# A decoder trunk in fp32: the seven-product scheme in one more pass of each MLP, with its products summed over passes and the SBUF tiles moved

## The chip, the core and the metric

The kernel runs on one NeuronCore of a Trainium2 chip. TensorE (PE in the profile) multiplies, VectorE (DVE) and ScalarE (ACT) work on tiles elementwise, GpSimd (POOL) does little here, and SyncE (SP) issues the DMAs that bring the weights from HBM. A tile is 128 partitions wide; PSUM, into which TensorE writes, has eight banks of 512 fp32 columns. The metric is the device time of one execution in microseconds. Before the change it is 2031.8 us, the median of three runs (2031.58 to 2032.2).

## The reference, cut to what matters

Sequence 256, width 2048, two layers. Layer 0 mixes with a gated short convolution, layer 1 with latent attention; each is followed by an MLP with 8192 hidden columns. All four blocks add to 1.414 times their input and are layer-normalised:

```python
def sq_relu_mlp(x, w1, w2):
    return jnp.square(jax.nn.relu(x @ w1)) @ w2

def reference(...):
    for layer in range(DEPTH):
        ...
        h = layer_norm(ALPHA * h + mix, ln_g[layer, 0], ln_b[layer, 0])
        h = layer_norm(ALPHA * h + sq_relu_mlp(h, mlp_w1[layer], mlp_w2[layer]),
                       ln_g[layer, 1], ln_b[layer, 1])
    return h
```

Everything is fp32. The kernel keeps that precision by splitting every operand into a rounded part (`hi`) and the rest (`lo`) and adding three products: hi by hi, hi by lo, lo by hi.

## The kernel before, in words

**Weights.** `stream` lists every piece of weight in the order of use, 512 KB each. `take` hands out the next piece and prepares those ahead of it, as long as no more than `LOOK` = 5 pieces lie ahead. `prepare` loads a piece on SP into one of five `raw` buffers, ScalarE rounds it to `hi` and VectorE subtracts to get `lo` (`split`, L116 and L117); there are eight `hi` and eight `lo` buffers. A pair of pieces for the seven-product scheme counts as three: VectorE first forms T1, T2, T3 and T4 from its blocks (L149, L152, L155), and four splits follow; T4 goes into the tile `t4` of the pool `fast`.

**An MLP** (`mlp`) runs in eight passes `q` over its hidden columns. A pass first makes eight chunks of 128 hidden columns: `products` runs 32 matmuls for each (`high` with 512 columns, L192, and `low` with 256, L196, output `ps_u`), `whole` adds the two halves of the PSUM tile, and `hidden` applies ReLU and square and splits into the tile `h` (SBUF tag `c`). Pass 0 instead takes the normalisation into the product (`mm_wide`, output `ps_w` and `ps_g`). Then the pass multiplies `h` with 1024 rows of the second weight and adds to `acc`, whose four blocks of 512 columns stand for two halves of the tokens (`block(n, t)`). `down` does this for one block of columns with 48 matmuls (`dot`, L276 to L278, output `ps_d`).

**The seven products.** In the passes of `FAST`, 1 to 6, the first two blocks of columns come from `down_fast` (output `ps_f`): seven products a step instead of eight, four steps of 21 matmuls each, 84 where two `down` would take 96. The left factors S1 to S4 are formed by VectorE in `hidden` and split into the tile `forms` (tag `a2`). `combine` then adds the seven PSUM tiles into `acc`, eleven VectorE instructions (L581, L650, L651) and one ScalarE copy.

**The last passes.** Pass 7 takes no seven products. In the first MLP it begins by preparing the residual for the next norm (`prepare_all`: sixteen VectorE instructions and one small product, `mu0p`), and ends in `to_wide`: after each block of columns its four chunks are transposed on TensorE (`turned`), added to the residual, counted for the statistics and split (`summed`); then come the first three products of the next stage (`group_of(3)`, `ps_g`), the statistics, and more products of that stage (`ps_w`). In the second MLP it ends in `to_out`: two blocks by `down`, the other two by `down_late`, which does the first half of the tokens entirely before the second. `finished` takes the statistics of each block (`bn_stats`) and, behind the last block of a half, normalises and stores that half. The gain and bias of the norm (`gbt`) are loaded on GpSimd's queue.

**Order and places.** Each engine's queue is written by the framework's planner, which gives every engine the earliest instruction in program order that its model holds to be ready; on the chip each queue then runs in that order. PSUM tiles come from two pools of four rotating banks. SBUF tiles lie one behind the other in the order in which pools and tags are first named: constants, then `xres`, `a1` and `a2` (16,512 bytes in each partition), `b` (33,024), `c` (16,384), S, Q and mu0 (1,024 each), `ab` (2,048), five `raw` buffers (4,096 each), eight `hi` and eight `lo` buffers (4,096 each), `tmp` (9,216), `small` (896), and the pool `fast` with `sf` (2,048) and `t4`.

Of the kernel before, what the change touches and what calls it, by code (L numbers as in the profile page):

```python
# [36 lines left out]
FAST = range(1, NQ - 1)  # L37
# [13 lines left out]
def trunk(ctx: ExitStack, tc: tile.TileContext, xT, vecs, w_first, w_in, w_out, w_kv, w_q, w_uk, w_uv,  # L51
# [9 lines left out]
    pmm = ctx.enter_context(tc.tile_pool(name="pmm", bufs=4, space=PS))  # L61
# [12 lines left out]
    def mlp_stream(l):  # L74
        out = []
        for q in range(NQ):
            out += halves(w1[l, q * QC:(q + 1) * QC])
            lead = 0
            if q in FAST:
                out += [(w2f[l, q, j, 0], w2f[l, q, j, 1]) for j in range(QC // 2)]  # L80
                lead = 2
            out += halves(w2[l, q, lead:])
        return out
# [6 lines left out]
    class Banks:  # L90
# [4 lines left out]
        @classmethod  # L95
        def open(cls, name):
            st = ExitStack()
            cls.more, cls.count = st.enter_context(tc.tile_pool(name=name, bufs=4, space=PS)), 0
            return st
# [30 lines left out]
    def prepare(i):  # L130
# [25 lines left out]
        f = state["fast"].tile([P, 2, BW], F32R, tag="t4", name=f"t4_{i}")  # L156
# [23 lines left out]
    def psum(name):  # L180
        return Banks.next().tile([P, 512], F32, tag="mm", name=name)
# [83 lines left out]
    def products(n, x, turned=None):  # L265

        for i in range(n):
            w = take()
            ps = psum("ps_u")
# [18 lines left out]
    def down(x, put, n):  # L288

        ps = [psum("ps_d") for _ in range(2)]  # L290
        for j in range(len(x) // 2):
            w, = take(1)
            for kk in range(2):
                k = 2 * j + kk
                for t in range(2):
                    dot(ps[t], wide_rows(w, kk), held(x[k], t), k == 0, k == len(x) - 1)
        for t in range(2):
            put(n, t, ps[t])

    def down_late(x, put, blocks):  # L300

        ws = {}
        for t in range(2):
            for n in blocks:
# [11 lines left out]
    def down_fast(x, forms):  # L316

        ps = {p: psum(f"ps_f{p}") for p, _, _ in FACTORS}
        n = len(x) // 2
        for j in range(n):  # L320
            b, = take(1)
            a = {"11": held(x[2 * j], 0), "12": held(x[2 * j + 1], 0), "22": held(x[2 * j + 1], 1)}
            for i in range(4):
                a[f"S{i + 1}"] = [forms[:, j, o, i * P:(i + 1) * P] for o in range(2)]
            for p, l, r in FACTORS:
                dot(ps[p], b[r], a[l], j == 0, j == n - 1)
        return ps
# [14 lines left out]
    cos_t = const.tile([P, T], F32, name="cos_t")  # L342
    sin_t = const.tile([P, T], F32, name="sin_t")
    mask_t = const.tile([P, 3 * P], F32, name="mask_t")
# [9 lines left out]

    def late_constants():
        nc.sync.dma_start(id_t, ident)
        nc.sync.dma_start(cos_t, cosT)
        nc.sync.dma_start(sin_t, sinT)
        nc.sync.dma_start(mask_t, mask)
# [145 lines left out]
    xres = act.tile([P, NC, T], F32, tag="xres", name="xres")  # L505
# [47 lines left out]
    late_constants()  # L553
# [3 lines left out]
    def mlp(idx, ln, blocks, fast, begin=None, extra=None):  # L557
# [24 lines left out]

        for q in range(NQ):
# [5 lines left out]
            if q == NQ - 1 and begin:  # L589
                begin()  # L590
            pair = []

            def hidden(m, ps, evac, *func):
                f = tmp.tile([P, T], F32, tag="fh", name="fh", bufs=3)
# [4 lines left out]
                put_split(h[m], f)  # L599
                pair.append(f)  # L600
                if forms is not None and m % 2:
                    (a11, a21), (a12, a22) = ((v[:, :P], v[:, P:]) for v in pair[-2:])
                    sf = fast.tile([P, 4, P], F32, tag="sf", name="sf")
# [459 lines left out]
```

## Time and profile before

| | us |
|---|---|
| median of three runs | 2031.80 |
| the profiled execution, its own time | 2031.86 |
| its span, first to last instruction | 2030.04 |
| TensorE busy | 2022.8 |
| VectorE busy | 1637.1 |
| ScalarE busy | 1186.2 |

The profile has one line for each group of instructions, with its engine, the tile written and read, the count and the mean duration. Matmuls overlap in it: one of 512 columns is shown for some 0.39 us, but the next starts 0.23 us later. What a matmul costs is therefore read from start to start in the timeline. `PEld` are the weight loads that go with each matmul.

### The profile page before, as it was taken

The page shows a single profiled execution, that of the slowest core. Times are in us where ns is not written, and L with a number is a line of the kernel's source. Part 1 is how long each engine was busy: PE and PEld are TensorE (multiplying, and loading weights), DVE is VectorE, ACT ScalarE, POOL GpSimd, SP SyncE. Part 2 cuts the span into 40 slices and gives each one's busy share as a digit, 9 for nine tenths or more (in the row PEclk, how much of TensorE's full clock was granted, in tenths as well). Part 3 has the DMA queues.
Part 4 walks back from the last instruction along what each step waited for, and adds up shares of the span by engine and source line. Part 5 has one row for each costly group of instructions (what it writes and reads, how often), then busy time and mean ns, then how long its engine had stood idle before and what let it go on. Part 6 is the DMA issues. An engine that isn't in the chain of part 4 may idle for free.

```text
span 2030.0 us, 30192 instructions
## 1 busy us (share of the span) xinstructions
PE 2022.8 (100%) x11240; PEld 1763.4 (87%) x11240; DVE 1637.1 (81%) x2559; ACT 1186.2 (58%) x1849; POOL 4.5 (0%) x25
## 2 busy tenths in 40 slices
PE   9999999999999999999999999999999999999998
PEld 8888888988888888888889998898888888888886
DVE  7667677778898988989788978776889898898966
ACT  6444445676566565655656655566656656565661
POOL 0000000000000000000000000000000000000000
PEclk9999999999999999999999999999999999999999
DMA  8666666564746557465654544656474664746573
GB/s 307 209 191 187 188 190 193 162 210 138 251 148 216 193 170 256 145 229 174 232 176 153 177 129 137 195 168 205 136 240 155 213 204 164 250 143 221 190 228 121
DMA packets 106851, 385.32 MB, mean 190 GB/s; under 512 B 11856, under 2 KB 12752, under 8 KB 106448
## 3 DMA queue, kind: packets, MB, share of 16 engines
q1 hardware_dynamic: 105984, 381.17, 57.9%
q0 software_dynamic: 576, 2.10, 0.3%
q8 instruction: 88, 1.44, 0.3%
q14 instruction: 59, 0.48, 0.1%
q10 hardware_dynamic: 144, 0.13, 0.0%
HBM read 381.25 MB, written 2.10 MB: 189 GB/s over the span
## 4 chain that ended last, share of the span: by engine, by line
PE 99%; DMA 0%; DVE 0%; issue 0%; SPq 0%; ACT 0%; DVEq 0%
PE ps_u L192 20%; PE ps_l L192 13%; PE ps_u L196 11%; PE ps_d L276 7%; PE ps_d L277 7%; PE ps_d L278 7%; PE ps_l L196 7%; PE ps_f L278 4%; PE ps_f L276 4%; PE ps_f L277 4%; PE ps_w L226 1%; PE ps_w L224 1%; PE ps_w L225 1%; PE ps_g L226 1%; PE ps_g L224 1%; PE ps_g L225 1%
## 5 line engine op out<-in xcount | busy, mean ns | idle before, releaser
L117 DVE TENSOR_TENSOR lo<-raw,hi 128x1024 fp32r<-128x1024 f32 x710 | 858.7, 1222 | 271.5 <-ACT hi L116 199.9
L116 ACT CAST hi<-raw 128x1024 fp32r<-128x1024 f32 x710 | 740.9, 1050 | 428.4 <-DMA raw<-in_w_dram 134.6
L192 PE MATMUL ps_u<-xhl,hi 128*128 128x512 f32 x1792 | 621.3, 391 | 0.0
L196 PE MATMUL ps_u<-xhl,lo 128*128 128x256 f32 x1792 | 500.1, 280 | 0.0
L192 PEld LDWEIGHTS ps_u<-xhl,hi 128*128 128x128 f32 x1792 | 334.4, 187 | 71.9
L196 PEld LDWEIGHTS ps_u<-xhl,lo 128*128 128x128 f32 x1792 | 339.2, 189 | 1.7
L276 PE MATMUL ps_d<-hi,h 128*128 128x512 f32 x640 | 249.9, 390 | 0.0
L277 PE MATMUL ps_d<-lo,h 128*128 128x512 f32 x640 | 249.3, 390 | 0.0
L278 PE MATMUL ps_d<-hi,h 128*128 128x512 f32 x640 | 249.2, 389 | 0.0
L192 PE MATMUL ps_l<-xhl_a,hi 128*128 128x512 f32 x704 | 244.1, 393 | 0.0
L196 PE MATMUL ps_l<-xhl_a,lo 128*128 128x256 f32 x704 | 195.5, 280 | 0.0
L192 PEld LDWEIGHTS ps_l<-xhl_a,hi 128*128 128x128 f32 x704 | 132.2, 188 | 29.8
L278 PEld LDWEIGHTS ps_d<-hi,h 128*128 128x128 f32 x640 | 120.2, 188 | 25.2
L276 PEld LDWEIGHTS ps_d<-hi,h 128*128 128x128 f32 x640 | 120.2, 188 | 25.0
L277 PEld LDWEIGHTS ps_d<-lo,h 128*128 128x128 f32 x640 | 120.2, 188 | 24.6
L196 PEld LDWEIGHTS ps_l<-xhl_a,lo 128*128 128x128 f32 x704 | 131.9, 188 | 0.2
L597 ACT ACTIVATE fh<-fh 128x256 f32<-128x256 f32 x112 | 46.5, 415 | 89.2 <-DVE fh L333 89.1
L116 ACT CAST hi_t<-raw_t 128x1024 fp32r<-128x1024 f32 x48 | 50.6, 1054 | 55.5 <-DVE raw_t L149 30.5
L192 PE MATMUL ps_l<-z,hi 128*128 128x512 f32 x240 | 82.4, 391 | 0.0
L226 PE MATMUL ps_w<-xd,hi 128*128 128x258 f32 x256 | 72.7, 285 | 0.0
L224 PE MATMUL ps_w<-xd,hi 128*128 128x258 f32 x256 | 72.6, 284 | 0.0
L225 PE MATMUL ps_w<-xd,lo 128*128 128x258 f32 x256 | 72.4, 283 | 0.0
(253 smaller groups left out, 3185.1 us busy)
## 6 DMA issues: line engine op xcount, KB each, us to landing
raw<-in_w_dram SPq DMA_DIRECT2D x416, 512.0 KB, 4.3
raw<-in_w2f_dram SPq DMA_DIRECT2D x96, 512.0 KB, 3.5
raw<-in_w_in_dram SPq DMA_DIRECT2D x88, 512.0 KB, 3.8
raw<-in_w_out_dram SPq DMA_DIRECT2D x32, 512.0 KB, 3.6
raw<-in_w_o_dram SPq DMA_DIRECT2D x32, 512.0 KB, 4.0
raw<-in_w_kv_dram SPq DMA_DIRECT2D x10, 512.0 KB, 3.6
raw<-in_w_q_dram SPq DMA_DIRECT2D x8, 512.0 KB, 4.4
raw<-in_w_uk_dram SPq DMA_DIRECT2D x8, 512.0 KB, 4.6
```

What stands on the lines that cost most here:

```text
L116: nc.scalar.copy(hi, src)
L117: nc.vector.tensor_tensor(lo, src, hi.bitcast(F32), ALU.subtract)
L192: nc.tensor.matmul(ps, w[blk // 8][0][:, blk % 8, :], x, start=first, stop=False)
L196: nc.tensor.matmul(ps[:, :T], w[blk // 8][1][:, blk % 8, :], x[:, :T], start=False, stop=last)
L224: nc.tensor.matmul(ps[:, :W], hi, x[k][:, :W], start=k == 0, stop=False)
L225: nc.tensor.matmul(ps[:, :W], lo, x[k][:, :W], start=False, stop=False)
L226: nc.tensor.matmul(ps[:, :W], hi, x[k][:, W:], start=False, stop=k == NC - 1)
L276: nc.tensor.matmul(ps, x[0], w[0], start=first, stop=False)
L277: nc.tensor.matmul(ps, x[0], w[1], start=False, stop=False)
L278: nc.tensor.matmul(ps, x[1], w[0], start=False, stop=last)
L597: nc.scalar.activation(f, f, AF.Relu)
```

## The change

`FAST` now takes in pass 7. The seven products of a pass are no longer combined in the pass: those that enter one block alone (2, 3 and 4) are added to `acc`, and the other four are kept in a new tile `sums`, added up over the passes 1 to 7; `fold` combines them once, in the last pass, with six VectorE instructions. The order of the seven products in a step is new, and every PSUM tile of the passes from 1 on has its bank written out. The forms and the splits of `h` are made for two chunks at a time. Preparing the residual is spread over the chunks of pass 7. In `to_wide` and `to_out` the first two blocks are ready after the fold, so that `down` and `down_late` do the other two; `gbt` is loaded on SP's queue. The tags of the large SBUF tiles are named at the start with unused columns between them, the cosine, sine and mask tables go to the attention's pool, and the region that the framework reserves for GpSimd's DMAs is cut to 4,096 bytes.

```diff
-FAST = range(1, NQ - 1)
+FAST = range(1, NQ)
...
+    xres = act.tile([P, NC, T], F32, tag="xres", name="xres")
+    for tag, columns in (("c", 4096), ("pad0", 64), ("b", 8256), ("a1", 4128), ("pad1", 96), ("a2", 4128), ("pad2", 96)):
+        act.tile([P, columns], F32, tag=tag, name=f"at_{tag}")
+    small.tile([P, 32], F32, tag="pad", name="at_pad", bufs=1)
...
-            return cls.more if cls.more is not None and cls.count % 8 >= 4 else pmm
+            return (cls.count - 1) % (4 if cls.more is None else 8)
...
-        f = state["fast"].tile([P, 2, BW], F32R, tag="t4", name=f"t4_{i}")
+        f = state["fast"].tile([P, 2, BW], F32R, tag="t4", name=f"t4_{i}", bufs=2)
...
-    def down(x, put, n):
+    def down(x, put, n, banks=(None, None), amid=None):
...
+            if amid and 2 * j + 2 == len(x) // 2:
+                amid()
...
-    FACTORS = (("4", "22", "T4"), ("2", "12", "21"), ("3", "S4", "22"), ("1", "11", "11"),
-               ("6", "S2", "T2"), ("7", "S3", "T3"), ("5", "S1", "T1"))
+    OWN, KEPT = ("1", "5", "7", "6"), (2, 3, 4, 5, 6, 7, 0)
+    FACTORS = (("3", "S4", "22"), ("1", "11", "11"), ("5", "S1", "T1"), ("7", "S3", "T3"),
+               ("2", "12", "21"), ("6", "S2", "T2"), ("4", "22", "T4"))
...
+        sums = fast.tile([P, 4, BW], F32, name=f"sums{idx}")
+        def keep(p, ps):
+            at = sums[:, OWN.index(p)] if p in OWN else block(*{"2": (0, 0), "3": (1, 0), "4": (0, 1)}[p])
+            if q == 0 or q == FAST[0] and p in OWN:
+                nc.scalar.copy(at, ps)
+            else:
+                nc.vector.tensor_tensor(at, at, ps, ALU.add)
+        def first_pair(h, forms, banks):
+            n = QC // 2
+            ps = {p: psum(f"ps_f{p}", bank) for (p, _, _), bank in zip(FACTORS, banks)}
+            for j in range(n):
+                fast_products(ps, h, forms, j, n)
+            for p in ps:
+                keep(p, ps[p])
+        def fold():
+            s1, s5, s7, s6 = (sums[:, i] for i in range(4))
+            both = acc[:, 1, :2 * BW].rearrange("p (b c) -> p b c", b=2)
+            right = acc[:, :, BW:2 * BW]
+            two = lambda v: v.unsqueeze(1).to_broadcast([P, 2, BW])
+            for d, a, b in ((block(0, 0), block(0, 0), s1), (s6, s6, s1), (block(1, 0), block(1, 0), s6),
+                            (s7, s7, s6), (both, both, two(s7)), (right, right, two(s5))):
+                nc.vector.tensor_tensor(d, a, b, ALU.add)
+                yield
...
-            if q == NQ - 1 and begin:
-                begin()
...
+                if begin:
+                    begin(range(1))
...
-                for m, ps in enumerate(products(QC, xhl, turned=None if q == NQ - 1 and begin else TURNED)):
+                for m, ps in enumerate(products(QC, xhl, TURNED, (0, 1))):
                     hidden(m, ps, whole)
+                    if q == NQ - 1:
+                        if begin:
+                            begin(range(max(2 * m, 1), 2 * m + 2))
             if q == NQ - 1:
-                blocks(block, put, h)
+                first_pair(h, forms, KEPT)
+                blocks(block, put, h, fold)
                 return
-            if q in FAST:
-                combine(put, down_fast(h, forms))
-            for n in range(2 if q in FAST else 0, NB):
-                if n == NB - 1 and extra:
-                    extra(block, q - 1)
-                down(h, put, n)
+            if q == 0:
+                for n in range(NB):
+                    down(h, put, n)
+            else:
+                first_pair(h, forms, KEPT)
+                for n, banks in ((2, (1, 2)), (3, (3, 4))):
+                    down(h, put, n, banks)
+                    if extra and n == 2 and q <= NB:
+                        for t in range(2):
+                            extra(block, q - 1, t, 5 + t)
...
-        for n in range(NB):
-            down(h, put, n)
-            if n:
-                turned(n - 1)
+        for _ in fold():
+            pass
+        down(h, put, 2, (1, 2))
+        turned(0)
+        down(h, put, 3, (3, 4), lambda: turned(1))
+        turned(2)
         ln.ws = group_of(GROUP)
...
-            nc.gpsimd.dma_start(gbt[:, n, :], gb[n].partition_broadcast(P))
+            nc.sync.dma_start(gbt[:, n, :], gb[n].partition_broadcast(P))
...
+        for _ in fold():
+            pass
         for n in range(2):
-            down(h, finished, n)
+            for t in range(2):
+                finished(n, t)
         down_late(h, finished, range(2, NB))
...
-    nc = _bacc.Bacc("TRN2", target_bir_lowering=False, num_devices=1)
+    nc = _bacc.Bacc("TRN2", target_bir_lowering=False, num_devices=1, dynamic_dma_scratch_size=4096)
```

More of the change, by code (lines that the diff above doesn't have):

```diff
@@ L178, in take, with psum @@
         return [ready.pop(i + j) for j in range(halves)]
-    def psum(name):
-        return Banks.next().tile([P, 512], F32, tag="mm", name=name)
+    def psum(name, bank=None):
+        bank = Banks.next() if bank is None else bank
+        return (pmm if bank < 4 else Banks.more).tile([P, 512], F32, tag=f"mm{bank}", name=name)
     def high_early(ps, w, blk, x, last):
@@ L552, in trunk @@
                 ln.prepare(k)
-    late_constants()
+    nc.sync.dma_start(id_t, ident)
     ln.widen("a1", "a2")
```

129 lines of the change are left out of this document (58 added, 71 removed).

## The prediction

> **What bounds the kernel now.** The page's busy times and its chain of waits came first:
>
> ```profile
> PE 2022.8 (100%) x11240; PEld 1763.4 (87%) x11240; DVE 1637.1 (81%) x2559; ACT 1186.2 (58%) x1849; POOL 4.5 (0%) x25
> ...
> PE 99%; DMA 0%; DVE 0%; issue 0%; SPq 0%; ACT 0%; DVEq 0%
> ```
>
> TensorE is the path from end to end, so work taken from other engines is worth nothing by itself; VectorE at 81% is near enough to become the path where work is pushed together. Next, busy times by stage: a seven-product part and the plain blocks behind it (pass 6, first MLP), the last pass of the first MLP (products, two blocks, two blocks with transposes, next stage), the last four blocks of the second MLP, and the tail. Columns: window, length, busy time of PE, PEld, DVE, ACT, POOL with counts, clock, DMA share, GB/s.
>
> ```profile
> 927.76:947.35 19.59, 19.59 (x86) 15.78 (x85) 18.15 (x24) 12.85 (x18) 0.53 (x1) 1.00 0.60 186
> 947.35:969.15 21.80, 21.80 (x97) 18.02 (x96) 19.09 (x23) 10.50 (x11) 0.00 (x0) 1.00 0.75 256
> 969.15:1013.97 44.82, 44.82 (x260) 39.55 (x259) 32.13 (x50) 27.45 (x46) 0.00 (x0) 1.00 0.67 223
> 1013.97:1035.77 21.80, 21.80 (x98) 17.98 (x97) 12.15 (x15) 9.84 (x13) 0.00 (x0) 1.00 0.63 193
> 1035.77:1060.12 24.35, 24.35 (x121) 20.47 (x120) 23.28 (x45) 15.04 (x25) 0.00 (x0) 1.00 0.50 162
> 1060.12:1080.42 20.30, 20.27 (x169) 20.06 (x168) 16.24 (x37) 9.66 (x22) 0.00 (x0) 1.00 0.42 144
> 1975.63:2019.19 43.56, 43.56 (x194) 36.07 (x193) 28.48 (x43) 10.98 (x14) 2.23 (x4) 1.00 0.36 133
> 2019.19:2030.00 10.81, 5.58 (x13) 2.00 (x11) 6.26 (x14) 0.20 (x1) 0.00 (x0) 1.00 0.26 97
> ```
>
> Seven products take 19.59 us for 84 matmuls, 233.2 ns each; two plain blocks 21.80 us for 96, 227.1 ns. VectorE has 18.15 of 19.59 us there, but only 12.15 of 21.80 in the last pass's first two blocks: that spare is what the change spends. Last, the timeline of TensorE and VectorE (start, duration, engine, line, tiles):
>
> ```profile
> 946.42 0.40 PE L278 MATMUL ps_f<-hi_t,forms 128*128 128x512 f32 x1
> 946.65 0.39 PE L276 MATMUL ps_f<-hi_t,forms 128*128 128x512 f32 x1
> 946.88 0.40 PE L277 MATMUL ps_f<-lo_t,forms 128*128 128x512 f32 x1
> 947.12 0.39 PE L278 MATMUL ps_f<-hi_t,forms 128*128 128x512 f32 x1
> ...
> 949.20 0.39 PE L278 MATMUL ps_d<-hi,h 128*128 128x512 f32 x1
> 949.43 0.39 PE L276 MATMUL ps_d<-hi,h 128*128 128x512 f32 x1
> 949.65 0.39 PE L277 MATMUL ps_d<-lo,h 128*128 128x512 f32 x1
> ```
>
> ```profile
> 945.25 0.68 DVE L581 TENSOR_TENSOR acc<-acc,ps_f 128x512 f32<-128x512 f32 x1
> ...
> 1035.47 1.28 DVE L581 TENSOR_TENSOR acc<-acc,ps_d 128x512 f32<-128x512 f32 x2
> ...
> 1055.20 2.36 DVE L117 TENSOR_TENSOR lo<-raw,hi 128x1024 fp32r<-128x1024 f32 x2
> ```
>
> From start to start a seven-product matmul takes 229 and 237 ns in turn, a plain one 226 to 227, after some ten matmuls of settling. VectorE's costs are read the same way: a second add of 512 columns adds 1.28 - 0.68 = 0.60 us, a second split of 1024 columns 2.36 - 1.22 = 1.14.
>
> **The change part by part**, against the profiled execution's 2031.86 us (the median of the runs is 2031.80).
>
> *Places in SBUF.* Nothing waits in the seven products, yet they pay 6 ns a matmul. What sets them apart is where operands start. Summing the tile sizes, `h` (tag c) and all hi and lo buffers agree modulo 512 bytes (16,384 + 3,072 + 2,048 + 20,480 = 82 x 512). `forms` in a2 is 128 bytes off (16,512 + 33,024 leaves 384), and `t4` 128 off (65,536 + 9,216 + 896 + 2,048 leaves 384). Stages whose operands keep one distance, `ps_d` and `ps_u`, run steadily. After the change a2 lies 130 x 512 bytes behind c and 83 x 512 ahead of hi, and `t4` 168 x 512 behind hi (65,536 + 7,168 + 1,024 + 8,192 + 2,048 + 2,048): all agree. b keeps its distance to hi, 256 modulo 512. So I take plain pace, 226.9 ns x 84 = 19.06 us, in the twelve parts there were: 12 x 0.53 = -6.4 us. Ends: no effect, or +6.9 us if all took the slowest spacing inside a step, 240 ns (500.25 to 500.49). The first stage reads a1 and a2, also 128 bytes apart today; its pairs settle within 2 ns of the steady 347: -0.2 us, between -0.8 and 0.
>
> *Last passes.* Two plain blocks, 96 x 226.9 = 21.78 us, become 19.06: 2 x -2.72 = -5.4 us. The last pass of the first MLP also gets the order of the others (44.57 against 44.39 us): -0.2. The small product of the residual, 0.24 us, only moves.
>
> *Kept sums.* Seven adds a pass in place of eleven and a copy: 2.4 us of VectorE less, nothing on the path, since TensorE already hid them. The written-out banks cost nothing in passes 1 to 6: the first sum is added before its bank is taken, and a product's bank comes up again 5.5 us after it ends, against 0.8 for its evacuation. Spreading sixteen preparations adds some 5 us to a VectorE that has 7 spare in the products' 44.4.
>
> *End of the first MLP.* Let T be the end of the last seven products. VectorE's list up to the statistics: two splits and seven adds, begun 2.1 us before T as at 945.25, end at T + 4.4. Then fold 4 x 0.60 + 2 x 1.14 = 4.7; ten splits 11.4; four adds of `ps_d` 2.4; four `summed` at 5.67 (1060.23 to 1065.90) 22.7: T + 45.6, and 0.8 to the statistics, 46.4. TensorE's own list is 21.8 + 4 x 0.79 (`turned`) + 17.4 (`ps_g`) = 42.4. Of the 4.0 us between, the 1.9 us of `ps_w` that the planner pulls ahead here today cover a part: +2.1 us. Ends: 0 if VectorE gains its lead earlier; 6 if two further splits go first and nothing covers. Queued behind the fold are the splits of the next weights, and TensorE waits for those (the sixth piece at T + 10.2 against its need at T + 14, the third unit of `ps_g` later than its need).
>
> *End of the second MLP.* VectorE again, from T + 4.4: fold 4.7; four `bn_stats` and two gains 3.6; three splits 3.4; add and statistics of the third block 1.4; the whole end of the first half 7.5 (2008.51 to 2016.02); add, statistics and gain of the second half 2.1: T + 27.1. The last add started today at 2019.39 and the span ended 10.65 later: T + 37.8. TensorE alone would allow 21.8 + 10.85 = T + 32.6. So +5.2 us. Ends: 0 if the splits slip in earlier and the lists overlap; 8 if `gbt`, 2 MB moved from GpSimd's queue to SP's among the weights' loads (9.5 us to landing today), makes those late. Storing, the tables moved to the attention's pool (0.5 MB, used 60 us later) and the smaller reserve hang on nothing late.
>
> Sum: -6.4 - 0.2 - 5.4 - 0.2 + 2.1 + 5.2 = -4.9, **2027.0 us**; own range 2023.5 to 2030.5 from the two ends.
>
> **The rivals.** (1) *VectorE's lists are hidden*: both ends as TensorE allows, 2027.0 - 7.3 = 2019.7, with half of them 2023. For: VectorE idles 7 us in each pass's products. Against: at most five pieces may be prepared ahead, so that idle time can't be used early.
>
> (2) *The tiles' places do nothing*: the seven products stay at 19.59. Then -2 x 2.19 - 0.2 + 7.3 = +2.7, 2034.6. For: no row shows an address, and the step also changes banks and left factors with every product. Against: `ps_g` changes banks as often and keeps its pace, and the seven products reach no steady spacing even over nine matmuls that all read `forms`. [...]
>
> (3) *The other side: the moved tiles unsettle the 1808 matmuls of 512 columns in `ps_u`, which read b.* The distance b to hi goes from 768 to 1792 modulo 2048; if that counts and not modulo 512, `ps_u` may fall into the spacing of the seven products: 1808 x 6.3 ns = 11.4 us, 2038.4. It ends the gain from 780 such matmuls on, and makes the kernel slower by over 0.2% from 1,430. Against: the left operands of `ps_d` lie at all four multiples of 512 within 2048, at one pace.
>
> **How the numbers follow.** 0.2%, 4.1 us, is about what a measurement of this kernel tells from no change. Forecast 0.50 (0.33 of it under 2027.7, the rest within), (1) 0.15, all faster, (2) 0.20, half of it over 2035.9 if the ends also cost more, (3) 0.12, slower, something else 0.03. Faster 0.48, within 0.28, slower 0.24. The range 2021.0 to 2035.5 leaves out (3) and the edges of (1) and (2).
>
> **What would show it.** Right: `ps_f` parts of about 19.06 us, fourteen of them; `ps_u` at 173.4 ns a matmul as now; VectorE without a gap behind the last seven products, TensorE waiting for `hi` or `lo` in `ps_g` and in the last blocks. Wrong: `ps_f` still at 233; `ps_u` or `ps_d` at another pace; TensorE waiting inside the seven products of pass 7, where loads or preparations would be late; or a tail as long as today's 10.8 us.

## The result and the profile after

The changed kernel takes 2037.8 us (median of eight runs, 2036.3 to 2041.4) against 2031.9 us (eight runs, 2031.6 to 2032.2): a ratio of 1.003, 95% interval 1.0021 to 1.004. It is slower by 0.3%, where 2027.0 us and a gain were forecast. The profiled execution is the shortest of the eight, 2036.3 us with a span of 2034.5; what lies between it and the median is taken up below, with the clock.

The page of the changed kernel, busy times and the sum of its chain of waits:

```profile
PE 2017.1 (99%) x11216; PEld 1758.5 (86%) x11216; DVE 1650.0 (81%) x2545; ACT 1188.0 (58%) x1813; POOL 2.3 (0%) x21
...
PE 93%; DVE 4%; DMA 1%; issue 1%; ACT 1%; SPq 0%; ACTq 0%; DVEq 0%
```

TensorE is busy 5.7 us less than before, as it should be with 24 matmuls fewer and a better pace, and the span is 4.5 us longer. It is no longer the chain from end to end: VectorE holds 4% of it, some 80 us, where it held none. The same stretches as before (columns as there: window, length, PE, PEld, DVE, ACT and POOL busy, clock, DMA share, GB/s); the last passes are split where T, the end of the last seven products, lies:

```profile
926.37:945.46 19.09, 19.09 (x87) 15.77 (x86) 18.04 (x25) 12.37 (x17) 0.00 (x0) 1.00 0.53 163
945.46:967.22 21.76, 21.76 (x98) 18.02 (x97) 18.83 (x21) 11.46 (x11) 0.00 (x0) 1.00 0.86 318
967.22:1011.61 44.39, 44.39 (x258) 39.13 (x257) 35.29 (x52) 27.57 (x45) 0.00 (x0) 1.00 0.51 156
1011.61:1030.69 19.08, 19.08 (x87) 15.77 (x85) 17.68 (x26) 12.41 (x18) 0.00 (x0) 1.00 0.54 160
1030.69:1055.42 24.73, 24.02 (x113) 19.39 (x112) 23.64 (x38) 13.45 (x18) 0.53 (x1) 1.00 0.62 209
1055.42:1084.08 28.66, 25.56 (x206) 24.50 (x205) 28.30 (x60) 15.20 (x32) 0.00 (x0) 1.00 0.52 175
1084.08:1116.78 32.70, 32.03 (x267) 31.64 (x265) 31.18 (x74) 24.73 (x51) 0.00 (x0) 1.00 0.50 157
1974.62:1993.70 19.08, 19.08 (x86) 15.77 (x85) 17.58 (x25) 12.26 (x16) 0.00 (x0) 1.00 0.80 276
1993.70:2017.78 24.08, 23.27 (x99) 18.11 (x98) 23.76 (x38) 4.41 (x5) 0.00 (x0) 1.00 0.12 49
2017.78:2034.50 16.72, 7.37 (x11) 2.42 (x9) 9.90 (x21) 0.20 (x1) 0.00 (x0) 0.78 0.33 125
```

A seven-product part is 19.08 us in pass 6 and in both last passes. Behind it, from 1030.69 on, VectorE is busy 23.64 of 24.73, 28.30 of 28.66 and 31.18 of 32.70 us, while TensorE falls short by 0.7, 3.1 and 0.7 us: VectorE is the bound there, as the experiments confirm. The last line has a granted clock of 0.78.

From start to start a seven-product matmul now takes 227 ns, with `h` and with `forms` alike (timeline of TensorE):

```profile
929.36 0.39 PE L284 MATMUL ps_f<-lo,h 128*128 128x512 f32 x1
929.59 0.39 PE L285 MATMUL ps_f<-hi,h 128*128 128x512 f32 x1
929.82 0.39 PE L283 MATMUL ps_f<-hi,forms 128*128 128x512 f32 x1
930.04 0.39 PE L284 MATMUL ps_f<-lo,forms 128*128 128x512 f32 x1
```

And the two places where the time was lost, in the timelines of VectorE and TensorE:

```profile
1071.64 5.76 DVE L122 TENSOR_TENSOR lo<-raw,hi 128x1024 fp32r<-128x1024 f32 x5
1077.31 0.75 DVE L491 TENSOR_TENSOR xres<-xres,turned 128x256 f32<-128x256 f32 x2
...
2021.42 0.68 DVE L578 TENSOR_TENSOR acc<-acc,ps_d 128x512 f32<-128x512 f32 x1
...
2025.14 5.49 PE L1000 MATMUL offset<-gbt,udiag 128*128 128x512 f32 x6 [5.48 <-DVE udiag L998]
2027.25 0.75 DVE L984 SCALAR_TENSOR_TENSOR acc<-acc,rr,offset 128x512 f32<-128x512 f32 x1 [1.51 <-PE offset L1000]
```

Five splits in a row stand ahead of the last transposed block (1077.31). At the very end the last add starts 3.6 us after the last `ps_d` (2017.78), TensorE waits 5.48 us, and the second half of its three `offset` products then takes 5.49 us. In the kernel before it took 2.84:

```profile
2023.12 2.84 PE L961 MATMUL offset<-gbt,udiag 128*128 128x512 f32 x6 [1.19 <-DVE udiag L959]
```

By stages of the two profiled executions (us; the forecast column puts the prediction's terms where they fall):

| stretch | before | after | difference | forecast |
|---|---|---|---|---|
| start to the first product on z | 274.43 | 273.65 | -0.78 | -0.2 |
| 512 products on z | 88.79 | 90.43 | +1.64 | 0 |
| up to the end of the last `ps_u`, first MLP | 650.74 | 647.53 | -3.21 | -3.4 |
| end of the first MLP, up to the first `ps_k` | 101.92 | 105.17 | +3.25 | -0.6 |
| attention and what follows it | 206.00 | 207.31 | +1.31 | 0 |
| up to the end of the last `ps_u`, second MLP | 653.75 | 650.53 | -3.22 | -3.2 |
| end of the second MLP | 54.41 | 59.88 | +5.47 | +2.5 |
| sum | 2030.04 | 2034.50 | +4.46 | -4.9 |

The passes gave what was forecast. Three stretches did not: both ends, with what follows the first, and the products on z.

### The profile page after: what moved, and what is told of

Its sections match the earlier page's. It is cut to its first block, busy times and chain, and to the rows that moved or that the text cites. A ratio compares the mean times of both kernels' runs of the same rounds, so it can differ in the third digit from the quotient of the medians.

```text
span 2034.5 us, 30102 instructions
## 1 busy us (share of the span) xinstructions
PE 2017.1 (99%) x11216; PEld 1758.5 (86%) x11216; DVE 1650.0 (81%) x2545; ACT 1188.0 (58%) x1813; POOL 2.3 (0%) x21
## 3 DMA queue, kind: packets, MB, share of 16 engines
q8 instruction: 88, 1.44, 0.3%
## 4 chain that ended last, share of the span: by engine, by line
PE 93%; DVE 4%; DMA 1%; issue 1%; ACT 1%; SPq 0%; ACTq 0%; DVEq 0%
PE ps_u L199 20%; PE ps_l L199 13%; PE ps_u L203 11%; PE ps_l L203 7%; PE ps_d L283 6%; PE ps_d L284 6%; PE ps_d L285 6%; PE ps_f L284 4%; PE ps_f L285 4%; PE ps_f L283 4%; DVE lo L122 1%; PE ps_w L233 1%; PE ps_w L232 1%; PE ps_w L231 1%; PE ps_g L231 1%
## 5 line engine op out<-in xcount | busy, mean ns | idle before, releaser
L283 PE MATMUL ps_d<-hi,h 128*128 128x512 f32 x576 | 224.8, 391 | 0.8 <-DVE sums L588 0.8
L285 PE MATMUL ps_d<-hi,h 128*128 128x512 f32 x576 | 224.3, 389 | 0.0
L284 PE MATMUL ps_d<-lo,h 128*128 128x512 f32 x576 | 224.2, 389 | 0.0
L283 PEld LDWEIGHTS ps_d<-hi,h 128*128 128x128 f32 x576 | 108.1, 188 | 23.8 <-ACT hi L121 1.6
L284 PEld LDWEIGHTS ps_d<-lo,h 128*128 128x128 f32 x576 | 108.1, 188 | 22.8 <-DVE lo L122 0.6
L285 PEld LDWEIGHTS ps_d<-hi,h 128*128 128x128 f32 x576 | 108.1, 188 | 22.5
L641 ACT ACTIVATE fp<-fp 128x256 f32<-128x256 f32 x112 | 46.7, 417 | 89.4 <-DVE fp L340 88.7
L121 ACT CAST hi_t<-raw_t 128x1024 fp32r<-128x1024 f32 x56 | 58.8, 1050 | 46.4 <-DVE raw_t L154 38.8
L154 DVE TENSOR_TENSOR raw_t<-raw,raw 128x1024 f32<-128x1024 f32 x56 | 68.3, 1220 | 8.1 <-DMA raw<-in_w2f_dram 8.0
L233 PE MATMUL ps_w<-xd,hi 128*128 128x258 f32 x256 | 72.9, 285 | 0.0
```

Source lines behind the costliest of these rows:

```text
L121: nc.scalar.copy(hi, src)
L154: nc.vector.tensor_tensor(t.rearrange(two, a=2), b12.unsqueeze(1).to_broadcast([P, 2, BW]), r1.rearrange(two, a=2), ALU.subtract)
L233: nc.tensor.matmul(ps[:, :W], hi, x[k][:, W:], start=False, stop=k == NC - 1)
L283: nc.tensor.matmul(ps, x[0], w[0], start=first, stop=False)
L284: nc.tensor.matmul(ps, x[0], w[1], start=False, stop=False)
L285: nc.tensor.matmul(ps, x[1], w[0], start=False, stop=last)
```

## The experiments

### The last passes, both, one and the other

Three kernels take the seven products out of both last passes, or of one. Only the set of passes differs (the empty one below, `(0,)` and `(1,)` for the other two), and where a last pass goes back to plain blocks the fold is spread over its chunks:

```diff
-FAST = range(1, NQ)
+FAST = [range(1, NQ if l in () else NQ - 1) for l in range(2)]
...
+                        if q not in passes:
+                            next(folding, None)
```

> The changed kernel with the seven products taken out of both last passes again; the kept sums, the written-out banks and the moved tiles stay, and the fold goes, one addition a chunk, into the products of pass 7. Theory A (both ends pay for the seven products there, by VectorE's list): the stages that the two traces share lose 0.78 + 3.28 + 3.28 + 0.43 us and gain 1.64 + 0.05 + 0.2 + 0.07, so 2031.86 - 5.8 = 2026.0 us, about 10 under the changed kernel's profiled 2036.3, and the ends stand as in the kernel before: about 101.9 us from the last ps_u of the first MLP to the first ps_k, 54.4 us behind the last ps_u of the second. Rival (the loss lies in the kept sums or the banks, not in the last passes): ends of 105 and 59 us as in the changed kernel, and 2036 + 5.4 = over 2035 us.

> The seven products in the last pass of the first MLP alone. Theory A, the two ends independent: 2026.0 + 3.26 (end of the first MLP) + 1.30 (first stages of the attention) = 2030.6 us, the end of the second MLP 54.4 us. Rival (the attention's 1.30 us comes from the moved tables or tiles and not from VectorE's backlog): 2029.3 here, and the 1.30 us stands in the kernel without either too. Rival (the profiled time is not typical: the runs of the changed kernel were 2036.3 to 2041.4): if that spread comes from the first end, this kernel shows it.

> The seven products in the last pass of the second MLP alone. Theory A: 2026.0 + 5.47 = 2031.5 us in the profiled execution, 59.9 us behind the last ps_u, a wait of 5.5 us of TensorE in the tail and a granted clock of 0.5 there; and if the clock in the tail makes the runs spread, this kernel spreads by some 5 us between runs and its median lies 1 to 2 us over its fastest. Rival (the spread is elsewhere): runs within 1 us.

| seven products in the last pass of | median (runs) us | first end | attention | second end |
|---|---|---|---|---|
| neither | 2026.36 (2026.16 to 2026.55) | 101.68 | 206.04 | 54.23 |
| the first MLP | 2032.34 (2031.30 to 2035.21) | 105.26 | 207.28 | 54.24 |
| the second MLP | 2032.06 (2030.27 to 2032.78) | 101.79 | 206.03 | 59.78 |
| both | 2037.77 (2036.3 to 2041.4) | 105.17 | 207.31 | 59.88 |

The kernel without them lies 0.4 us from the expected 2026.0 and is faster than before (ratio 0.9972, 0.9961 to 0.9982). The profiled executions of the other two, 2031.3 and 2032.06, meet 2030.6 and 2031.5 within 0.7. The ends are independent and add up; the kept sums, the banks and the places are not what costs. The attention's 1.3 us comes and goes with the first end, so it is VectorE's backlog and not the moved tables; 1.0 us of it is a wait of TensorE for a tile of VectorE's (`kqva`) that the kernel before and the one with neither don't have. The stretches of the kernel with neither, from the last `ps_u` of the first MLP to the statistics and from the last `ps_u` of the second MLP to the last `ps_d`, show TensorE almost without a gap:

```profile
1011.89:1078.48 66.59, 66.56 (x384) 58.40 (x383) 51.86 (x95) 34.77 (x59) 0.00 (x0) 1.00 0.53 166
1970.14:2013.70 43.56, 43.56 (x194) 36.04 (x193) 28.46 (x43) 10.99 (x14) 0.00 (x0) 1.00 0.37 133
```

VectorE has 14.7 us spare in the first and 15.1 in the second: that was the cover that the change spent. The spread between runs was expected of the second end; the first one has the larger (3.9 against 2.5 us), and the kernel without either has 0.4. With the first end alone, six runs of 2031.30 to 2032.34 have a mean granted clock of 1.000 and five of 2033.38 to 2035.21 one of 0.999.

### The clock in the tail

```diff
             for i, ps in enumerate(offsets):
                 nc.tensor.matmul(ps, negative, gbt[:, i, BW:], start=True, stop=False)
+            idle = psum("idle")
+            for _ in range(6):
+                nc.tensor.matmul(idle, negative, block(0, 0), start=True, stop=True)
```

> The changed kernel with six more fp32 products of 512 columns into a bank that nobody reads, behind the last ps_d and ahead of the offset products, some 0.85 us each: TensorE's 5.5 us of waiting are filled. Theory C (the clock that fell to 0.5 at 2023.7 us makes the offset products 1.71 us each in place of 0.82): the clock stays at 1.0, last add to end takes about 10.6 us in place of 13.1, 2036.3 - 2.5 = 2033.8 us, and the runs spread by 1 us or less. Rival (the wait itself is the cost, the clock only a sign of it): 2036.3 us or more, with the spread as it was.

The timeline of the kernel with the tail kept busy:

```profile
2025.72 2.84 PE L1003 MATMUL offset<-gbt,udiag 128*128 128x512 f32 x6
2026.89 2.46 DVE L984 SCALAR_TENSOR_TENSOR acc<-acc,rr,offset 128x512 f32<-128x512 f32 x3 [0.56 <-PE offset L1003]
```

The offset products are back at 2.84 us without any work being taken away (granted clock 1.00 from 2018.37 to 2028.60, where the changed kernel has 0.50 from 2023.70 to 2030.52), last add to end of span is 10.5 us in place of 13.1, the profiled execution 2034.25 (2033.8 was expected, the last add being 0.5 us later), the median 2035.52 (2034.19 to 2038.91), 2.25 us under the changed kernel's. So the slow clock behind the wait cost some 2 us. The spread stayed, 4.7 us where 1 was expected; it is not made in the tail alone, as the kernels above say too.

A second kernel takes work from VectorE ahead of the tail in place of filling TensorE's wait; it leaves out the normalisation of the first half of the tokens:

```diff
             if t == 0:
                 rsqrt(r, ve)
                 for i in range(NB):
-                    centred(i)
-                    scaled(i, us[i], gbt[:, i, BW:])
+                    store(t, i)
                 return
```

> The changed kernel, storing the first half of the tokens without its normalisation (that half of the output is left out): 8 x 0.69 = 5.5 us less on VectorE ahead of the last add. Theory B for the second end: the last add begins right behind the last ps_d, 43.9 us behind the last ps_u in place of 46.8, 2.9 us earlier, and TensorE's wait for udiag falls from 5.5 to 2.6 us. Theory C: a wait of 2.6 us leaves the clock at 1.0, another 2.5 us: last ps_u to end 56.0 - 5.4 = 50.6 us, 2031 us in the fastest runs. Rival to C (any wait of that size halves the clock): 53.1 us and 2033.4 us.

Timeline of that kernel:

```profile
2020.37 0.69 DVE L578 TENSOR_TENSOR acc<-acc,ps_d 128x512 f32<-128x512 f32 x1 [1.24 <-PE ps_d L285]
...
2024.10 2.84 PE L999 MATMUL offset<-gbt,udiag 128*128 128x512 f32 x6 [2.05 <-DVE udiag L997]
```

The last add now waits for the last product (43.72 us behind the last `ps_u`, not 46.80), TensorE's wait is 2.05 us, the granted clock is 1.00 from 2020.65 to 2026.94, and the stretch to TensorE's last instruction is 50.29 us in place of 56.01: the forecast 50.6. The median is 2032.69 us (2031.50 to 2034.68), its profiled execution 2032.63 with a granted clock of 0.98 on the mean from 1071.53 to 1141.53. Note 50.29: the kernel before has 50.33. Even with 5.5 us of VectorE's work left out the seven products win nothing at this end.

### VectorE's list in the first end

Three kernels change it: less work, another order, another engine. The first leaves out the sums of the statistics for all chunks but one.

```diff
-            nc.vector.tensor_tensor(self.S, self.S, d, ALU.add)
-            nc.vector.tensor_tensor(self.Q, self.Q, sq, ALU.add)
+            if self.idx != 1:
+                nc.vector.tensor_tensor(self.S, self.S, d, ALU.add)
+                nc.vector.tensor_tensor(self.Q, self.Q, sq, ALU.add)
```

> The changed kernel, with the sums S and Q of the second layer's first statistics left out but for the first chunk: thirty additions of 256 columns less on VectorE, 30 x 0.33 = 9.9 us, between the last seven products of the first MLP and the statistics; the normalisation that follows is not the reference's. Theory B (VectorE's list sets that end): the last ps_u to the first ps_k takes about 101.92 - 2.72 = 99.2 us in place of 105.17, the attention behind it 206.0 in place of 207.3, and 2036.3 becomes about 2029, with runs that spread by 1 us. Rival (ScalarE's copies or the weights' loads set it, VectorE only waits with them): 104 us or more, 2035 us.

Statistics at T + 41.1 in place of T + 53.4, first end 101.11 us, attention 206.04, profiled execution 2030.64, median 2031.05 (2030.10 to 2032.55). That is theory B, with 1.6 us less gain than put down. The stretches from T to the statistics and from there to `ps_k`:

```profile
1031.00:1072.12 41.12, 39.15 (x237) 34.32 (x236) 38.47 (x58) 24.36 (x40) 0.53 (x1) 1.00 0.65 215
1072.12:1113.03 40.91, 40.91 (x344) 40.91 (x343) 37.88 (x86) 30.65 (x64) 0.00 (x0) 1.00 0.55 180
```

Behind the statistics TensorE has no gap left; ahead of them it still waits 2.0 us, 0.8 of it for the fold (`turned <- DVE acc`) and 1.0 for a `lo`. These 2.0 us are what keeps 101.1 from 99.2.

The order: `take` with two pieces prepared ahead for these three units in place of `LOOK`, so that three splits move behind the statistics.

```diff
-        ln.ws = group_of(GROUP)
+        ln.ws = group_of(GROUP, 2)
```

> The changed kernel, where at the end of the first MLP the three units of the next stage (ps_g) are taken with two pieces prepared ahead in place of five: three splits of 1024 columns, 3 x 1.15 = 3.5 us of VectorE, leave the list ahead of the last transposed block; they come right behind the statistics. Theory B in its first form (the order of VectorE's list counts: what stands ahead of the last summed): statistics at T + 50 in place of T + 53.4, last ps_u to first ps_k 105.2 - 3.4 = 101.8 us, about 2033 us in the fastest runs. Theory B in its second form (the amount of VectorE's work up to ps_k counts, 31.18 us of the 32.70 between the statistics and ps_k being busy): statistics 3.4 us earlier, ps_k at most 1.5 us, over 2034.5 us. In both TensorE's wait of 1.5 us ahead of the last four chunks gets shorter, and with it the granted clock should stay at 1.0 there in every run.

Statistics at T + 50.8, 2.6 us earlier, and yet the first `ps_k` 1.3 us later (106.51 us), the median 2038.77 (2037.98 to 2040.63). The second form holds, and worse: the moved splits are wanted at once. TensorE's waits between the last seven products and the end of the projections, in the kernel with two pieces ahead (total, times, longest):

```profile
PE ps_w L232 <- DVE lo L122: 2.5, 1, 2.5
...
PE ps_g L231 <- ACT xd L426: 1.1, 3, 0.5
```

and the same in the changed kernel:

```profile
PE ps_g L231 <- ACT xd L426: 2.2, 3, 1.5
...
PE ps_w L232 <- DVE lo L122: 0.6, 1, 0.6
```

The wait for the last transposed block shrank from 1.5 to 0.5 us and one for `lo` grew from 0.6 to 2.5. Another order of a list that leaves no spare time moved the wait here.

The other engine:

```diff
-            nc.vector.tensor_tensor(self.Q, self.Q, sq, ALU.add)
+            (nc.gpsimd if self.idx == 1 else nc.vector).tensor_tensor(self.Q, self.Q, sq, ALU.add)
```

> The changed kernel with the fifteen additions to Q at the end of the first MLP on GpSimd in place of VectorE: 15 x 0.33 = 5.0 us less on VectorE. No row of the traces has a GpSimd addition; at up to four times VectorE's 0.33 us it would hide, since a chunk takes 1.4 us, and the last one would add up to 1 us ahead of the statistics. Theory B: statistics at about T + 49, last ps_u to first ps_k 101 to 102 us in place of 105.17, 2032 to 2033 us. Rival (GpSimd and VectorE hold each other up at SBUF): VectorE's additions and splits beside it take longer, and 105 us or more stay.

The first end takes 109.55 us, the median is 2041.77 (2040.57 to 2042.62): 4.0 us slower than the changed kernel, though VectorE has fifteen instructions less. Groups of instructions between 1030 and 1085 us in this kernel (GpSimd's from 1000 to 1100 us; behind the bar busy us, mean ns):

```profile
L410 POOL TENSOR_TENSOR Q<-Q,sq 128x256 f32<-128x256 f32 x15 | 14.4, 961 | 26.5 <-ACT sq L408 25.9
...
L427 DVE SCALAR_TENSOR_TENSOR xd<-xres,vec,xd 128x256 fp32r<-128x256 f32 x15 | 10.2, 680 | 1.3 <-ACT xd L426 1.3
L409 DVE TENSOR_TENSOR S<-S,xres 128x256 f32<-128x256 f32 x14 | 9.1, 648 | 0.0
```

and in the changed kernel:

```profile
L427 DVE SCALAR_TENSOR_TENSOR xd<-xres,vec,xd 128x256 fp32r<-128x256 f32 x16 | 7.7, 482 | 1.1 <-ACT xd L426 1.1
...
L409 DVE TENSOR_TENSOR S<-S,xres 128x256 f32<-128x256 f32 x15 | 6.3, 418 | 0.0
```

On the mean these two go from 418 to 648 and from 482 to 680 ns: 14 x 0.23 + 15 x 0.20 = 6.2 us, more than the 15 x 0.33 = 5.0 us that were taken away. The timeline, VectorE first and then GpSimd, shows some of them:

```profile
1057.79 1.22 DVE L122 TENSOR_TENSOR lo<-raw,hi 128x1024 fp32r<-128x1024 f32 x1
1058.93 0.95 DVE L427 SCALAR_TENSOR_TENSOR xd<-xres,vec,xd 128x256 fp32r<-128x256 f32 x1
1059.80 0.94 DVE L409 TENSOR_TENSOR S<-S,xres 128x256 f32<-128x256 f32 x1
1060.66 0.47 DVE L427 SCALAR_TENSOR_TENSOR xd<-xres,vec,xd 128x256 fp32r<-128x256 f32 x1
...
1057.86 2.60 POOL L410 TENSOR_TENSOR Q<-Q,sq 128x256 f32<-128x256 f32 x2 [2.40 <-ACT sq L408]
```

The two that begin within the 2.60 us of the GpSimd additions take 0.95 and 0.94 us; the next, which begins behind them, takes 0.47. The split at 1057.79 takes 1.22 us as in the changed kernel, though GpSimd began beside it, and all seventeen splits have a mean of 1217 ns against 1218. The two additions that begin beside that split take 2.60 us together, where two of the mean length would take 1.92. An instruction with an operand in PSUM (`xres<-xres,turned`) has a mean of 414 ns in both kernels. The rival holds for VectorE's additions (418 to 648 ns) and not for its splits; what in the hardware lengthens the one and not the other wasn't shown. This profile's first end also has a stretch of half clock (0.96 on the mean from 1031.71 to 1071.71), behind a wait of TensorE (below); half of 3.41 us, 1.7 us, is an estimate of its share in the 4.4 us that this end is longer.

### Places in SBUF

Three kernels, each with one operand of the matmuls moved against the rest: `forms`, `b`, `t4` (two lines that replace that of the changed kernel, and one left out). With `b` moves `a1`, and with `t4` the other tiles of its pool, which no matmul reads:

```diff
-    ... ("pad0", 64), ("b", 8256), ("a1", 4128), ("pad1", 96), ("a2", 4128), ("pad2", 96)):
+    ... ("pad0", 64), ("b", 8256), ("a1", 4128), ("a2", 4128), ("pad2", 192)):
+    ... ("b", 8256), ("a1", 4128), ("pad1", 32), ("a2", 4128), ("pad2", 96)):
-    small.tile([P, 32], F32, tag="pad", name="at_pad", bufs=1)
```

> The changed kernel with the unused columns in front of a2 put behind it instead: a2, and so forms, moves by 384 bytes, and no other tile. Theory P (the distance of forms to h and hi modulo 512 sets the pace of the seven products): a part goes from 19.08 us back towards 19.6 us, all fourteen, since 48 of its 84 matmuls read forms; 14 x 0.3 to 14 x 0.5 us = 4 to 7 us longer in all, ps_u and ps_d unchanged at 44.39 and 21.76 us. Rival (the new order of the seven products and their written-out banks made the pace): 19.08 us stays.

> The changed kernel without the 32 unused columns in the pool small: t4, with the rest of the pool fast, moves by 128 bytes, and no other tile. Theory P, with forms alone off at 19.48 us and both off at 19.59 in the kernel before: t4, which 12 of 84 matmuls read as their right operand, is worth 0.11 us of a part, 19.08 + 0.11 = 19.19 us, 1.5 us over fourteen parts. Rival (t4 has no effect; the rest of the 19.59 is from the order of the products): 19.08 us.

> The changed kernel with b moved by 256 bytes (no unused columns in front of it, fewer in front of a2), so that b lies at 0 modulo 512 from hi and lo in place of 256; a1 moves with it, all else stays. Theory P as the prediction had it (only a changing distance costs, a constant one doesn't): ps_u stays at 44.39 us, 173.4 ns a matmul, and the products on z stay at 176.6. Rival (the third of the prediction in a milder form, the constant distance counts too): ps_u or the z products change their pace; every ns is 1.8 us over ps_u and 0.5 us over z.

| | `ps_f` part | `ps_u` | products on z |
|---|---|---|---|
| changed kernel | 19.08 | 44.39 | 90.43 |
| forms 128 bytes off | 19.48 | 44.39 | 88.79 |
| t4 128 bytes off | 19.22 | 44.39 | 90.43 |
| both off (kernel before) | 19.59 | 44.39 | 88.79 |
| b at 0 in place of 256 modulo 512 | 19.08 | 44.39 | 90.43 |

The two shares add up: 19.08 + 0.40 + 0.14 = 19.62 against 19.59, though order and banks of the products differ between the two kernels. In the timeline of the kernel with forms off the even 0.23 us is gone, 0.22 to 0.24 from start to start, where `h` is read as well as where `forms` is:

```profile
1030.18 0.39 PE L283 MATMUL ps_f<-hi,h 128*128 128x512 f32 x1
1030.41 0.39 PE L284 MATMUL ps_f<-lo,h 128*128 128x512 f32 x1
1030.63 0.40 PE L285 MATMUL ps_f<-hi,h 128*128 128x512 f32 x1
1030.87 0.40 PE L283 MATMUL ps_f<-hi,forms 128*128 128x512 f32 x1
1031.11 0.40 PE L284 MATMUL ps_f<-lo,forms 128*128 128x512 f32 x1
```

The constant distance, 0 or 256, made no difference to `ps_u` (44.39 us) nor to z (90.43). A changing distance was tried at 128 bytes alone; that distances count modulo 512 bytes was the author's estimate, and no run shows it. Each was run once (2042.36, 2040.48 and 2038.65 us); the readings above are of stages without waits and repeat from pass to pass within 0.01 us.

### The products on z

```diff
-    summed(ln, chain(products(1, z), lagged(NC - 1, z)), residual)
+    summed(ln, chain(products(1, z, TURNED), lagged(NC - 1, z)), residual)
```

> The kernel without seven products in the last passes, and the first product on z takes its third block low before high, as ps_u does in every pass. Theory Z (the pace of the alternating 512 and 256 columns is a matter of how the row of matmuls is entered: ps_u, entered so, runs at 173.4 ns, z at 176.6): the z products take 88.8 us in place of 90.43, 2026.36 - 1.64 = 2024.7 us. Rival (z's address sets its pace): 90.4 us and 2026.4 us.

Median 2024.77 us (2024.15 to 2024.89), z 88.89 us: theory Z. z kept its address in the kernel with forms off, too, and ran at the quick pace there (88.79 us), with the order of z's products as in the changed kernel: what differs is the stage ahead, which reads the moved a2. Timeline of the changed kernel, 0.36 and 0.35 us from one pair to the next:

```profile
299.64 0.40 PE L199 MATMUL ps_l<-z,hi 128*128 128x512 f32 x1
299.88 0.28 PE L203 MATMUL ps_l<-z,lo 128*128 128x256 f32 x1
300.00 0.40 PE L199 MATMUL ps_l<-z,hi 128*128 128x512 f32 x1
300.24 0.28 PE L203 MATMUL ps_l<-z,lo 128*128 128x256 f32 x1
300.35 0.40 PE L199 MATMUL ps_l<-z,hi 128*128 128x512 f32 x1
```

With one `low` ahead of its `high` at the start the same row settles at 0.347 us a pair for all that follows, 173.6 ns a matmul over the whole row. This kernel is the best of all: 0.9965 of the time before (0.9952 to 0.9977).

### What the runs of the first end differ by

The kernel with b at 0 was profiled with a slow first end, 107.37 us, though its instructions there are those of the changed kernel. Two windows of it:

```profile
1077.84:1081.25 3.41, 1.47 (x12) 1.43 (x12) 2.90 (x9) 2.47 (x5) 0.00 (x0) 1.00 0.95 342
1081.25:1084.66 3.41, 3.41 (x18) 3.41 (x17) 3.41 (x10) 1.52 (x4) 0.00 (x0) 0.50 0.42 172
```

In the first TensorE idles 1.94 us ahead of the last four chunks of `ps_g`; in the second the clock is 0.5, and eighteen matmuls touch it where at 0.12 us apart some 28 would. In these traces the clock changes in steps of 3.413 us: in the changed kernel's it is at 1.0 from 6.42 to 2023.70 (591 steps), then at 0.5 for 6.83 us and at 1.0 for 3.41; here it is at 0.5 for 3.41. Call one such step, counted from a fall, a cell. In the first end the clock fell in five profiles, behind a cell in which TensorE had idled 1.71 us (half of the second end's normalisation left out), 1.73 (`forms` moved), 1.91 (`t4` moved), 1.94 (`b` at 0) and 3.07 (`Q` on GpSimd). In the changed kernel's profile the wait of 1.5 us lies across the edge of two cells, 0.81 and 0.70, and the clock did not fall.

The waits with a fall were longer than this one, but a longer wait was not always followed by a fall. In the kernel with two pieces ahead a wait of 2.5 us, 1.1 and 1.4 in two cells, had none. In the kernel that leaves out half of the normalisation, these are the cell with the wait in the first end and the two that share the wait of 2.05 us in the tail:

```profile
1076.96:1080.37 3.41, 1.70 (x14) 1.49 (x13) 3.13 (x9) 2.47 (x5) 0.00 (x0) 1.00 1.00 334
2019.03:2022.44 3.41, 3.02 (x10) 1.50 (x8) 2.07 (x6) 0.13 (x1) 0.00 (x0) 1.00 0.00 0
2022.44:2025.86 3.42, 1.76 (x4) 0.87 (x5) 2.65 (x8) 0.07 (x1) 0.00 (x0) 1.00 0.08 32
```

Behind the first, with 1.71 us idle, the clock fell; behind the others, with 0.39 and 1.65, it did not.

With the fall the first end takes 106.96 to 107.48 us in three kernels with the changed kernel's instructions there (half of the second end's normalisation left out, `b` at 0, `t4` moved), and without it 105.14 to 105.26 in three others (the changed kernel, the one with the tail kept busy, the first MLP alone): 1.8 to 2.3 us more, of which up to 0.4 is the longer wait itself. Why the wait is longer in some executions stays open. The fall fits the runs with the first end alone and their two clocks, and would explain why the median lies 1.5 us over the profiled execution; the profiles of those slower runs aren't there to show it, and a kernel with the waits of the first end filled wasn't tried.

## Why the prediction was wrong

**Places in SBUF: right.** Forecast -6.4 for the twelve parts, measured 12 x 0.51 = -6.1, and 0.04 more per pass from `ps_d`; fourteen parts of 19.08 us against 19.06 forecast. Rival 2 falls with the two kernels that move `forms` and `t4`: 128 bytes cost 0.40 and 0.14 us a part. What in the hardware does it stays open; the runs show only that a distance that changed from matmul to matmul cost this much, and that the constant one, 0 or 256, left `ps_u` at 44.39 us and z at 90.43.

**Last passes, order of the last pass: right.** Two parts of 19.08 against 21.80, and 44.39 us.

**Kept sums, banks, moved tables, smaller reserve: right** in that the kernel with these and without seven products in the last passes gains 5.6 us, against a forecast of 6.4 + 0.2 + 0.2 less the 1.64 us on z, 5.2.

**End of the first MLP: the step that failed, mis-sized.** The term was +2.1 us, with 6 as its end. Against 101.92 - 2.72 = 99.2 it measured +6.0, and +1.3 more in the attention. The mechanism was named rightly, VectorE's list up to the statistics; its length was not. T + 46.4 was forecast, T + 53.4 measured. Ten splits were counted ahead of the last transposed block, fourteen stood there (4 x 1.15 = 4.6 us). That the planner put them there because they were ready while `summed` waited is likely, but no run shows it. VectorE also waited 2.7 us itself, which the sum had at nothing: 1.3 for ScalarE's `hi`, 1.1 for its `xd` and 0.3 for its `sq`. Together that is 7.3 us against the 7.0 missing. And the term stopped at the statistics: behind them VectorE is busy 31.18 of 32.70 us, so what comes late there stays late into the projections. The experiment with two pieces ahead says that the count of splits ahead is not the whole: with three fewer the statistics came 2.6 us earlier and `ps_k` later all the same. What the sum lacked was the work of VectorE up to `ps_k`. Of the 6.0 us, gaps of TensorE in the trace make 4.5; the other 1.5 lie in matmuls that follow each other more slowly there (`ps_g` every 127 ns against 122 before), in part, by the author's estimate, because a matmul is shown for 0.28 us there and the next starts 0.12 us later, so that a wait is shown shorter than it is.

**End of the second MLP: mis-sized too, by a step that wasn't in it.** The list was right to 0.6 us: the last add at T + 27.7, forecast T + 27.1. What followed was taken over from the trace of before, 10.65 us, and took 13.1. The prediction had VectorE late by 5 us and did not ask what TensorE does meanwhile: it idles 5.5 us and comes back at a granted clock of 0.50 (2023.70 to 2030.52), 2.4 us. Against 54.41 - 2.72 the term measured +8.2, its end being 8, though the reason given for that end, weights made late by `gbt` on SP's queue, isn't seen: VectorE waits 1.4 us for `hi` around T there and 1.3 us at the same place of the first end, where no `gbt` is loaded. TensorE also waits 0.8 us for a bank of the seven products (`ps_d` for the add of `sums`), where no cost had been put; it is no part of the 8.2, since the last add starts 3.6 us behind the last product anyway.

**The products on z: not in the sum.** +1.64 us. Rival 3 foresaw a slower spacing in such a row of alternating 512 and 256 columns, but by the distance of `b`, in `ps_u`, and of 11.4 us. `ps_u` kept 173.4 ns, and `b` moved by 256 bytes changed neither row. z's row took 90.43 us as it was entered and 88.89 with one pair swapped at its start, at the same address. That rival 3's 2038.4 us lies so near to the 2037.8 measured is luck.

**Rival 1**, that the lists are hidden, was wrong. It agrees with the reason given against it that VectorE still had 9.1 us spare in the products of pass 7 (35.29 busy of 44.39) and was full right behind them; a kernel that prepares more pieces ahead wasn't tried. With one part of the list left out, 101.11 us are reached at the first end and 50.29 up to TensorE's last instruction at the second, only 0.6 and 0.04 better than the 101.68 and 50.33 without the seven products. Leaving these parts out doesn't bring their 2.72 us a pass back.

In sum the forecast -4.9 became +4.46 by +5.2 (first end and attention: 7.3 in place of 2.1), +3.0 (second end: 8.2 in place of 5.2), +1.6 (z), and -0.4 of small terms; the median adds 1.5 us, probably by the clock in the first end.

**The range.** Both ends came out at or over the largest values that the prediction gave them, 6 and 8. With both its sum would have been 2033.7 us, beyond the 2030.5 of its own range, though within the 2035.5 that it gave with the rivals: it took them as if they would not be long together, though both rest on one thing, how much work VectorE finds behind the last seven products.

## What to carry to other kernels

Before saving TensorE work in a stage, count the other engines' work up to the point where the stage's result is used, and on past it until they have a spare; where they are already full, a saving turns into waiting, and neither of the remedies tried here, another order of the splits and GpSimd for some additions, helped. When TensorE is going to wait, ask how long: a wait of 1.7 us was paid a second time in clock here, where 1.71 us of it fell into one step of 3.41 us and the granted clock was 0.5 in the next. Operands that a row of matmuls takes in turn did best here where all lay at one distance modulo 512 bytes (19.08 us a part, against 19.48 and 19.22 with one of them 128 bytes off), and a long regular row is worth a look at its spacing, since one swapped pair at its start gave 1.6 us here.

## What the runs showed of the hardware

- The granted clock was 1.0 or 0.5 in the changed kernel's trace and changed in steps of 3.413 us (1.0 for 591 steps, 0.5 for two, 1.0 for one). The falls seen stood behind a cell with 1.71, 1.73, 1.91, 1.94 and 3.07 us of idle time of TensorE in the first end, and 3.41 in the tail of the changed kernel. There was none behind 0.39, 0.70, 0.81, 1.1, 1.4 and 1.65 us, nor behind 1.87 us in the tail of the kernel with `forms` off, unless some matmul records are missing there. No run was made to find a limit between them.
- The clock came back behind a cell without idle time (3.41 us busy of 3.41 in the first end of the kernel with `b` at 0, 3.42 of 3.42 in the tail of the changed kernel) and stayed down behind one with 1.44 us idle (1.97 busy of 3.41, the same tail): it was down for 3.41 us in the one and for 6.83 us in the other.
- A GpSimd addition of 256 columns took 961 ns on the mean of fifteen. In the stretch with them, VectorE's instructions of that size with all operands in SBUF took 648 and 680 ns on the mean in place of 418 and 482, those with an operand in PSUM 414 ns in both kernels, and the splits 1217 ns against 1218.
- 512 matmuls of one stage, with the same operands and addresses, took 173.6 ns each (88.89 us) with one pair swapped at the start of the row and 176.6 ns (90.43 us) without.
